# A one-layer attention and convolution trunk: the sums of a seven-product matrix form made earlier, a norm moved to other engines, and convolution taps ordered behind splits

## Chip, cores and metric

The kernel runs on one core of one Trainium2 chip. The metric is the device time of one execution in microseconds (us); three runs of the kernel before give a median of 1469.73.

## What is computed

One layer of a decoder on x of 1024 tokens x 1024 channels, in float32:

```python
h = rms_norm(x, attn_norm)
z = h @ w_in                                   # conv (512), q (768), six k/v parts (256 each), gates (36)
conv_out = conv_mixer(a_conv, ...)             # GLU, causal depthwise conv of width 31, LayerNorm, swish
kc, vc = compress(kc_r, ...), compress(vc_r, ...)
nsa_out = nsa_attention(q, kc, vc, ks, vs, kw, vw, gates)   # compressed, selected and window branches
x = x + concat([conv_out, nsa_out]) @ w_out
h = rms_norm(x, ffn_norm)
gate, up = split(h @ w_gate_up)                # 2 x 2816
x = x + (silu(gate) * up) @ w_down
return rms_norm(x, final_norm)
```

## The kernel before

**Products.** Every float32 product is made of three TensorE (PE) matmuls. Each operand is split into a high part, a cast by ScalarE (ACT), and a low part, the difference from it. `load_w` (L214) loads a weight tile, casts it (L225) and lets GpSimd (POOL) make the low part in four pieces of 128x256 (L229). `split` (L232) does the same for activations, with the subtraction on VectorE (DVE, L233). [...]

**Stages.** The 1024 tokens are worked in two halves of 512. First come the norm and the input projections of the first half: value projections, convolution input, compression of keys and values, queries. Two chains of side work run along there on DVE: the 31 convolution taps for each of two channel tiles (`conv_taps`, `cacc` at L601, fed by `taps_in`) and the splits and gates of the projections. Then attention runs, woven with fill work: the second half's projections, and the first half's output projection and feed-forward pairs. The feed-forward width of 2816 is 22 blocks of 128, worked as 11 pairs. A pair in the old form is `up_part` (four `gu` tiles of 24 matmuls, L1184, with `af` and `aw` made behind them at L1191 and L233) and `down_part` (eight `dn` tiles of 6 matmuls, L1203, each added to x by DVE at L1208).

**Around the change.** When attention is done, `second` makes the second half's output projection (`wo`, L1139, its weights loaded by `out_loads_k` at 256 KB each, ACT cast at L1065, POOL subtraction at L1068) and its feed-forward norm (`ffn_norm_in`: square on ACT, `rs` on DVE and POOL, the product x * rs * weight on DVE at L241, then PE transposes `tp` and their splits into `h`). It is woven with the first half's pairs. The first half's remaining pairs follow, and the second half's pair 0 in the old form. Its pairs 1 to 10 use a seven-product form (Winograd's variant of Strassen's): `wino_up` makes one block of gate and one of up from seven products of 256 tokens instead of eight (L1331, PSUM tiles `yy`, `zz`, `aa`). It needs four sums of quarters of h (`terms`, L1256 to L1263, each then split into `term`) and, for each block, four sums of weight quarters (`sum`, L1290), which `cut` splits into `w_s` (L1277; `w_g` is the split of the weight itself). `c` (L1346) is a sum of yy and a copy of zz; DVE must have made it before the next product goes on adding to yy. Between the products stand down matmuls of the pair before, six at a time.

The `terms` and the first `sum` tiles are written behind the last old-form pair of the first half; the scheduler places five of nine term operations ahead of it. Two buffers are used in turn, so that a sum waits for the split of the one before. Ahead of the first seven-product tile stand 36 down matmuls (`down_lead`, L1217: the first six of pair 0's eight tiles, interleaved).

**What sets the order.** PE's order in the seven-product form is written by hand. Elsewhere a list scheduler with its own time model places the instructions; `weave` mixes two generators by estimated durations, and `tc.issue_after` puts what follows behind a named instruction. On each engine the placed order is fixed, and an engine waits in it.

Of the kernel before, what the change touches and what calls it, by code (L numbers as in the profile page):

```python
# [19 lines left out]
P = 128  # L20
# [68 lines left out]
def tile_hymba(ctx: ExitStack, tc, x, attn_norm, w_in, conv_w, conv_b, conv_ln_g, conv_ln_b,  # L89
# [124 lines left out]
    def load_w(parts, a, b, eng=pool):  # L214
# [14 lines left out]
            eng.tensor_sub(lo[:, q], raw[:, q], hi[:, q].bitcast(F32))  # L229
        return (hi[:, :n].rearrange("p (k c) -> p k c", k=a), lo[:, :n].rearrange("p (k c) -> p k c", k=a))  # L230

    def split(hi, lo, src):  # L232
        return act.copy(hi, src), dve.tensor_sub(lo, src, hi.bitcast(F32))  # L233

    def norm_rows(dst, src, grow, p, tmp):
# [3 lines left out]
        dve.tensor_scalar(rs, ss, 1.0 / DM, EPS, op0=ALU.mult, op1=ALU.add)
        pool.tensor_tensor(rs, rs, mhalf, op=ALU.pow)  # L240
        dve.scalar_tensor_tensor(dst, src, rs, grow, op0=ALU.mult, op1=ALU.mult)  # L241
# [215 lines left out]
    def project_d(feed, dst, row, halves, scaled=False):  # L457
        wh, wl = feed.get()
        for hf in halves:
            o = acc_bank("zo")  # L460
            yield from gemm_t(o, wh, wl, hf)
            zh = p1.tile([P, 512], F32R, tag="zh", name="zh", bufs=2)
            zl = p1.tile([P, 512], F32R, tag="zl", name="zl", bufs=2)
            if scaled:
                sc = qsc[:, row // P:row // P + 1]
                act.mul(zh, o, sc)
                dve.scalar_tensor_tensor(zl, o, sc, zh.bitcast(F32), op0=ALU.mult, op1=ALU.subtract)
            else:
# [470 lines left out]

    def taps_in(n):  # L940
        taps = conv_taps(0)
        for _ in taps:
            yield n


# [111 lines left out]
            for kq in range(2) for ch in range(2) for c in range(2)]  # L1057

    def out_loads_k(p):
        def load(kt, ch):  # L1060
            raw = p.tile([P, 512], F32, tag="oraw", name="o_raw")
            hi = p.tile([P, 512], F32R, tag="ohi", name="o_hi", bufs=2)
            lo = p.tile([P, 512], F32R, tag="olo", name="o_lo", bufs=2)
            sp.dma_start(raw, w_out[0, kt * P:(kt + 1) * P, ch * 512:(ch + 1) * 512])
            act.copy(hi, raw)  # L1065
            for c in (0, 256):
                q = slice(c, c + 256)
                pool.tensor_sub(lo[:, q], raw[:, q], hi[:, q].bitcast(F32))  # L1068
            return hi, lo
        return [lambda kt=kq * 4 + k, ch=ch: load(kt, ch) for kq in range(2) for ch in range(2) for k in range(4)]  # L1070
# [83 lines left out]
    def ffn_norm_in(si, tag):  # L1154
        grow, xns = norm_space(acts[si])
        load_row(grow, ffn_norm[0])
        for t, x1 in enumerate(x1s[si]):
            xn = xns[t % 3]
            norm_rows(xn, x1, grow, pools[si], xn)
            yield 4.0  # L1160
            transpose_tile(xn, h2[si][0], h2[si][1], t * P, tag)
            yield 0.9

    banks, splits = [0], []
# [77 lines left out]
    def half(si, w, kh, th):  # L1242
        return h2[si][w][kh][:, :, th * 256:(th + 1) * 256]

    def wino_terms(si, p, tmp):
        def val(w, kh, th):
            return half(si, w, kh, th).bitcast(F32)
        x, y = (tmp[:, i, :].rearrange("p (k t) -> p k t", k=4) for i in range(2))

        def term(src):  # L1250
            h, l = [p.tile([P, 4, 256], F32R, tag="term", name="term", bufs=8) for _ in range(2)]
            split(h, l, src)
            return h, l

        def less(dst, src, kh, th):
            dve.tensor_sub(dst, src, val(0, kh, th))  # L1256
            dve.tensor_sub(dst, dst, val(1, kh, th))

        def from_(dst, kh, th, src):
            dve.tensor_sub(dst, val(0, kh, th), src)  # L1260
            dve.tensor_tensor(dst, dst, val(1, kh, th), op=ALU.add)

        dve.tensor_tensor(x, val(0, 0, 1), val(1, 0, 1), op=ALU.add)  # L1263
        less(y, x, 0, 0)
        t1 = term(y)
        from_(y, 1, 1, y)
        t2 = term(y)
        from_(x, 1, 1, x)
        t3 = term(x)
        from_(y, 1, 0, y)  # L1270
        t4 = term(y)
# [27 lines left out]
    def wino_load(f, p, q, raws=None, sums=None):  # L1299
        if raws is None:  # L1300
            raw = wp.tile([P, WCH], F32, tag="raw", name="g_raw", bufs=2)[:, :KT * P]
            raws = wino_raw(f, raw.rearrange("p (k c) -> p k c", k=KT),
                            (p, last["p"])[f % 2 == 0].tile([P, KT, P], F32, tag="uraw", name="u_raw"))
# [60 lines left out]
    def wino_ffn(fps, p, terms, ahead, down, behind):  # L1364
        loads = [lambda f=2 * fp + f2: wino_load(f, p, pd) for fp in fps for f2 in range(2)][1:]

        def down_load(f, own):
            if own:
                return load_w([(0, w_down[0, f * P:(f + 1) * P, :])], 1, DM, dve)
            raw = wp.tile([P, WCH], F32, tag="raw", name="d_raw", bufs=2)[:, :DM]  # L1370
            sp.dma_start(raw, w_down[0, f * P:(f + 1) * P, :])
            return [x.rearrange("p (o k) c -> p o (k c)", o=1)
                    for x in cut(p, raw.rearrange("p (k c) -> p k c", c=P), "g", 2)]
        for fp in fps:
            aws = new_aws((1,))
            wd = []
            for f2 in range(2):
                if loads:
                    with issue_after(behind):
                        ahead.append(loads.pop(0)())  # L1380
                    behind = []
                end = fp == fps[-1] and f2 == 1
                wd.append(down_load(2 * fp + f2, not end))
                wino_up(ahead.pop(0), terms, aws[1], f2, down, p, ALL, (6, 3, 3) if end else (6, 6, 6))
            run(down)
            down = down_part(wd, (1,), ALL, aws, fp == fps[-1])
        run(down)

# [45 lines left out]
    def fill_all():  # L1434
# [21 lines left out]
        for _ in range(NF // 2):  # L1456
            yield from ffn(feed, (0,), FT)

    def second(p):
        set_in(1, p)  # L1460
        set_norm(1, p)
        yield from out_proj_k(Feed(out_loads_k(p), 2), 1, ALL[:6])
        yield from ffn_norm_in(1, "t")

    BUFS = dict(k=1, v=1, q=2, pr=9, ph=3)
    def conv_rest():
# [4 lines left out]
    with ExitStack():  # L1471
# [15 lines left out]
    raws = wino_raw(2, base[:, :KT * P].rearrange("p (k c) -> p k c", k=KT),
                    last["p"].tile([P, KT, P], F32, tag="uraw", name="u_raw"))
    terms = wino_terms(1, last["p"], tmp)
    sums = list(wino_sums(*raws, pd))  # L1490
# [22 lines left out]
    p5_stack.close()
    pd_stack.close()
# [30 lines left out]
```

## Time and profile before

| what | us |
|---|---|
| three runs | 1472.3, 1466.56, 1469.73 (median 1469.73) |
| the profiled execution | 1464.45 |
| its span, first to last instruction | 1462.7 |
| PE busy in it | 1425.4 (97%) |
| DVE, ACT, POOL busy | 1029.5, 771.1, 698.5 |
| mean granted clock of PE | 0.994 |

The profiled execution is 5.28 us below the median of the runs, and 1.75 us of it lie outside the span. Rows of a timeline give start and duration in us, engine, line, operation and tiles; a bracket at the end gives the idle time before it and who ended it. A group's row gives a duration in ns. A mean over rows of a helper line such as L233 mixes many tiles.

### The profile page before, as it was taken

The numbers are of one execution on the slowest core, as the hardware profiler recorded it, in microseconds if no ns is written. First come the engines' busy times: TensorE is split into PE (matmuls) and PEld (weight loads), VectorE is DVE, ScalarE is ACT, GpSimd is POOL, SyncE is SP. The second block draws the span as 40 slices with busy tenths as digits, with TensorE's granted clock in tenths as the row PEclk, the third lists the DMA queues.
The fourth block names the chain that finished last, engine by engine and source line by source line (L and its number), as shares of the span: only waits on it lengthen the run. The fifth ranks groups of instructions, "written<-read, shape, count | busy, mean of one in ns | idle before, by whom it ended". The sixth has DMA issues, their size and how long they took to land.

```text
span 1462.7 us, 23496 instructions
## 1 busy us (share of the span) xinstructions
PE 1425.4 (97%) x7995; PEld 1231.0 (84%) x7995; DVE 1029.5 (70%) x2280; ACT 771.1 (53%) x1603; POOL 698.5 (48%) x977
## 2 busy tenths in 40 slices
PE   8999999999999999999999999999999999999997
PEld 7888888987778888888888888787887899999996
DVE  6893586779686768777587785412638988788884
ACT  6323566768675666766666664322425444444443
POOL 5677574767675546655665556645568000000001
PEclk9999999999999999999999999999999999999999
DMA  7236488567597244335335213734244423223311
GB/s 234 75 117 205 129 237 254 155 196 208 163 285 220 72 109 113 90 94 136 92 100 138 81 41 104 217 123 144 80 130 155 134 87 115 87 87 116 115 60 72
DMA packets 234246, 196.34 MB, mean 134 GB/s; under 512 B 14745, under 2 KB 204029, under 8 KB 234126
## 3 DMA queue, kind: packets, MB, share of 16 engines
q1 hardware_dynamic: 234126, 194.84, 45.1%
q8 instruction: 63, 1.03, 0.3%
q14 instruction: 57, 0.47, 0.1%
HBM read 161.04 MB, written 33.75 MB: 133 GB/s over the span
## 4 chain that ended last, share of the span: by engine, by line
PE 72%; DVE 9%; DMA 7%; POOL 6%; ACT 3%; issue 2%; SPq 1%; POOLq 0%; ACTq 0%; DVEq 0%
PE gu L1184 17%; PE dn L1203 14%; PE yy L1331 8%; PE pt L845 5%; PE zz L1331 4%; PE wo L1118 3%; POOL w_lo L229 3%; PE zo L145 3%; PE o L863 3%; PE s L818 3%; PE o L862 3%; DVE cacc L601 2%; PE vo L145 2%; DMA w_raw<-in_w_in_dram 2%; DMA o_raw<-in_w_out_dram 2%
## 5 line engine op out<-in xcount | busy, mean ns | idle before, releaser
L229 POOL TENSOR_TENSOR w_lo<-w_raw,w_hi 128x256 fp32r<-128x256 f32 (+1 forms) x508 | 411.9, 844 | 161.2 <-ACT w_hi L225 154.0
L1184 PE MATMUL gu<-h,w_hi 128*128 128x512 f32 x768 | 253.0, 398 | 0.6 <-DVE x L1208 0.6
L1203 PE MATMUL dn<-w_hi,aw 128*128 128x512 f32 x656 | 230.7, 397 | 1.6 <-DVE x L1208 1.2
L225 ACT CAST w_hi<-w_raw 128x1024 fp32r<-128x1024 f32 (+1 forms) x147 | 152.5, 1050 | 131.8 <-DMA w_raw<-in_w_in_dram 44.1
L839 POOL TENSOR_SCALAR pr<-pr,l,gates 128x640 f32<-128x640 f32 (+5 forms) x192 | 149.1, 791 | 119.2 <-DVE l L834 94.2
L233 DVE TENSOR_TENSOR pl<-pt,ph 128x384 fp32r<-128x384 f32 x264 | 140.3, 551 | 55.2 <-ACT ph L233 53.5
L829 ACT ACTIVATE pr<-pr,m 128x640 f32<-128x640 f32 (+5 forms) x192 | 141.4, 737 | 71.4 <-DVE m L826 69.6
L1184 PEld LDWEIGHTS gu<-h,w_hi 128*128 128x128 f32 x768 | 143.2, 188 | 29.5 <-DVE x L1208 1.0
L233 ACT CAST ph<-pt 128x384 fp32r<-128x384 f32 x264 | 118.6, 478 | 76.9 <-PE pt L845 60.4
L1413 POOL TENSOR_TENSOR rs<-rs,mhalf 128x1 f32<-128x1 f32 x4 | 2.6, 645 | 320.4 <-DVE rs L1412 320.2
L1184 PE MATMUL gu<-h,w_lo 128*128 128x512 f32 x384 | 152.3, 397 | 0.0
L1203 PEld LDWEIGHTS dn<-w_hi,aw 128*128 128x128 f32 x656 | 123.1, 188 | 27.5 <-DVE x L1208 2.1
L1208 DVE TENSOR_TENSOR x<-dn,x 128x512 f32<-128x512 f32 x168 | 113.4, 684 | 42.0 <-PE dn L1203 41.4
L845 PE MATMUL pt<-ident,pr 128*128 128x128 f32 x792 | 137.9, 274 | 2.3 <-DVE pl L233 1.2
L1203 PE MATMUL dn<-w_lo,aw 128*128 128x512 f32 x328 | 129.6, 395 | 0.0
L826 DVE CUSTOM_DVE_ANT_0 pr<-s,base 128x384 f32<-128x384 f32 (+3 forms) x192 | 101.2, 533 | 33.9 <-PE s L822 21.4
L845 PEld LDWEIGHTS pt<-ident,pr 128*128 128x128 f32 x792 | 102.2, 141 | 20.0 <-POOL pr L839 2.8
L145 PE MATMUL zo<-h,w_hi 128*128 128x512 f32 x320 | 106.0, 399 | 1.5 <-ACT w_hi L225 0.7
L1277 ACT CAST w_s<-sum 128x512 fp32r<-128x512 f32 x80 | 49.3, 621 | 108.3 <-PE yy L1331 90.5
L818 PE MATMUL s<-kt,q 128*128 128x384 f32 (+3 forms) x288 | 101.4, 354 | 3.6 <-DMA q<-q_d 1.6
L862 PE MATMUL o<-ph,vt 128*128 128x384 f32 x264 | 98.7, 374 | 2.3 <-ACT ph L233 1.9
L1331 PEld LDWEIGHTS yy<-term,w_s 128*128 128x128 f32 x720 | 93.8, 189 | 8.3 <-DVE c L1346 3.4
(275 smaller groups left out, 3156.9 us busy)
## 6 DMA issues: line engine op xcount, KB each, us to landing
w_raw<-in_w_gate_up_dram SPq DMA_DIRECT2D x48, 512.0 KB, 3.7
w_raw<-in_w_down_dram SPq DMA_DIRECT2D x43, 512.0 KB, 3.5
w_raw<-in_w_in_dram SPq DMA_DIRECT2D x40, 512.0 KB, 4.2
u_raw<-in_w_gate_up_dram SPq DMA_DIRECT2D x20, 512.0 KB, 4.9
g_raw<-in_w_gate_up_dram SPq DMA_DIRECT2D x19, 512.0 KB, 3.9
qc<-q_d SPq DMA_DIRECT2D x32, 192.0 KB, 3.9
pc_d<-pct SPq DMA_DIRECT2D x16, 384.0 KB, 3.7
pct<-pc_d SPq DMA_DIRECT2D x32, 192.0 KB, 2.7
```

Source lines behind the costliest of these rows:

```text
L145: lastpe[0] = pe.matmul(*args, **kw)
L225: act.copy(hi[:, :n], raw[:, :n])
L229: eng.tensor_sub(lo[:, q], raw[:, q], hi[:, q].bitcast(F32))
L233: return act.copy(hi, src), dve.tensor_sub(lo, src, hi.bitcast(F32))
L818: pe.matmul(sv, q2[0], kk_[:, 0, kk], start=True, stop=False)
L829: act.activation(pr[:, :n], pr[:, :n], AF.Exp, bias=m, scale=-1.0, accum_out=l3[:, r:r + 1])
L839: pool.tensor_scalar(x_, x_, l3[:, r2:r2 + 1], gates[:, i, c:c + 1], op0=ALU.mult, op1=ALU.mult)
L845: pe.transpose(pt[:, r * P:(r + 1) * P], prs[st][1 + r][:, kk * P:(kk + 1) * P], ident)
L862: pe.matmul(o[:, :384], v, ph, start=False, stop=False)
L1184: pe.matmul(o, w[:, k, :], h2[si][h][k // 4][:, k % 4, :], start=n == 0, stop=n == 3 * KT - 1)
L1203: pe.matmul(o, aws[si][:, a, k, t * P:(t + 1) * P], b[:, 0, ch * 512:(ch + 1) * 512], start=n == 0, stop=n == 5)
L1331: pe.matmul(o, w[:, k, :], h[:, k, :], start=fresh and n == 0, stop=n == 11, skip_group_check=not fresh)
```

## The change

It has five parts.

1. **Sums early.** `wino_terms` no longer splits: it makes four separate sums, in tiles of the second half's `act` space. It is called with the first weight sums from a new function `ahead_of_form`, ahead of the first half's last pair. The splits (`wino_split`) stay where they were.
2. **Second norm.** For the second half, DVE's one product of x, rs and the weight is replaced by an ACT multiplication by rs and a POOL multiplication by the weight row, both 128x1024. The row is loaded at the start of `second`, into a tile of its own.
3. **Output weights** are loaded in pairs of k tiles (512 KB), in turn into the `uraw` buffer and `base`.
4. **Taps.** Each step of the first half's taps is ordered behind the latest low part of a split, or the latest `zl` of a projection.
5. **Start of the form.** `down_lead` isn't used: the down matmuls of pair 0 follow the first products six at a time. The down weights of pair 1 are loaded when those are through, and fewer loads stand ahead.

The diff, cut:

```diff
+    lastlo = [None]
+
     def split(hi, lo, src):
-        return act.copy(hi, src), dve.tensor_sub(lo, src, hi.bitcast(F32))
+        pair = act.copy(hi, src), dve.tensor_sub(lo, src, hi.bitcast(F32))
+        lastlo[0] = pair[1]
+        return pair
...
-        dve.scalar_tensor_tensor(dst, src, rs, grow, op0=ALU.mult, op1=ALU.mult)
+        if aside:
+            act.mul(dst, src, rs)
+            pool.tensor_mul(dst, dst, grow)
+        else:
+            dve.scalar_tensor_tensor(dst, src, rs, grow, op0=ALU.mult, op1=ALU.mult)
...
         taps = conv_taps(0)
-        for _ in taps:
+        while True:
+            with tc.issue_after(lastlo[0].ins):
+                if next(taps, None) is None:
+                    return
             yield n
...
         def load(kt, ch):
-            raw = p.tile([P, 512], F32, tag="oraw", name="o_raw")
+            if kt % 2 == 0:
+                if kt % 4 == 0:
+                    pair = p.tile([P, 2, 512], F32, tag="uraw", name="o_raw")
+                else:
+                    pair = base[:, :DM].rearrange("p (k c) -> p k c", k=2)
+                sp.dma_start(pair, w_out[0, kt * P:(kt + 2) * P, ch * 512:(ch + 1) * 512]
+                             .rearrange("(k p) c -> p k c", p=P))
+                pairs.append(pair)
+            raw = pairs[-1][:, kt % 2, :]
...
-            sp.dma_start(raw, w_out[0, kt * P:(kt + 1) * P, ch * 512:(ch + 1) * 512])
...
-        x, y = (tmp[:, i, :].rearrange("p (k t) -> p k t", k=4) for i in range(2))
+        t3, t1, t2, t4 = [tmp[:, i, :].rearrange("p (k t) -> p k t", k=4) for tmp in tmps for i in range(2)]
...
+        dve.tensor_tensor(t3, val(0, 0, 1), val(1, 0, 1), op=ALU.add)
+        less(t1, t3, 0, 0)
+        from_(t2, 1, 1, t1)
+        from_(t3, 1, 1, t3)
+        from_(t4, 1, 0, t2)
+        return t1, t2, t3, t4
...
-                if loads:
+                if loads and len(ahead) < 2:
...
-                wd.append(down_load(2 * fp + f2, not end))
+                if fp != fps[0]:
+                    wd.append(down_load(2 * fp + f2, not end))
...
             run(down)
+            if fp == fps[0]:
+                ahead.append(loads.pop(0)())
+                wd = [down_load(2 * fp + f2, True) for f2 in range(2)]
...
+    def ahead_of_form():
+        assert not out_left
+        early["raws"] = wino_raw(2, base[:, :KT * P].rearrange("p (k c) -> p k c", k=KT),
+                                 pd.tile([P, KT, P], F32, tag="uraw", name="u_raw"))
+        early["terms"] = wino_terms(1, [acts[1].tile([P, 2, DM], F32, tag="act", name="terms", bufs=2)
+                                        for _ in range(2)])
+        with issue_after(normed):
+            early["sums"] = list(wino_sums(*early["raws"], pd))
...
+        grow = py.tile([P, 2, 542], F32, tag="y", name="grow").rearrange("p a b -> p (a b)")[:, :DM]
+        load_row(grow, ffn_norm[0])
...
-    with issue_after([gone] + splits):
-        ahead = [wino_load(2, p4, pd, raws, sums)]
+    behind = [gone] + splits
+
+    with issue_after([gone]):
+        ahead = [wino_load(2, p4, pd, early["raws"], early["sums"])]
...
-        down = down_lead(wd, 1, aws)
-        some(down, 36)
-        wino_ffn(range(1, NF // 2), p4, terms, ahead, down, [gone] + splits)
+        down = down_part(wd, (1,), ALL, aws)
+        wino_ffn(range(1, NF // 2), p4, terms, ahead, down, behind)
```

**DVE behind the second norm.** The place is the end of the second half's transposes, beside the first half's pair 9 (L1191 `af` and `aw` of its two blocks; `h_11222` to `h_11225` are the second half's normed rows, high and low). Before:

```order
L233 TENSOR_TENSOR aw<-af,aw 128x512
L233 TENSOR_TENSOR h_11224<-tp,h_11222 128x4x128
L233 TENSOR_TENSOR h_11225<-tp,h_11223 128x4x128
L1263 TENSOR_TENSOR terms<-h_11222,h_11224 128x1024
L1256 TENSOR_TENSOR terms<-terms,h_11222 128x1024
L1257 TENSOR_TENSOR terms<-terms,h_11224 128x1024
L1260 TENSOR_TENSOR terms<-h_11223,terms 128x1024
L1261 TENSOR_TENSOR terms<-terms,h_11225 128x1024
L1191 TENSOR_TENSOR af<-gu,af 128x512
L233 TENSOR_TENSOR aw<-af,aw 128x512
L1208 TENSOR_TENSOR x_5749<-dn,x_5749 128x512 x4
L1208 TENSOR_TENSOR x_5750<-dn,x_5750 128x512 x4
```

After (L235 is the split, L1275 to L1282 are the terms, L1313 the weight sums):

```order
L235 TENSOR_TENSOR aw<-af,aw 128x512
L1282 TENSOR_TENSOR terms<-h_11222,h_11224 128x1024
L235 TENSOR_TENSOR h_11225<-tp,h_11223 128x4x128
L1313 TENSOR_TENSOR sum<-u_raw 128x512
L1313 TENSOR_TENSOR sum<-base,u_raw 128x512
L1275 TENSOR_TENSOR terms<-terms,h_11222 128x1024
L1313 TENSOR_TENSOR sum<-sum,base 128x512
L1276 TENSOR_TENSOR terms<-terms,h_11224 128x1024
L1279 TENSOR_TENSOR terms<-h_11223,terms 128x1024
L1313 TENSOR_TENSOR sum<-base,sum 128x512
L1279 TENSOR_TENSOR terms<-h_11223,terms 128x1024
L1280 TENSOR_TENSOR terms<-terms,h_11225 128x1024
```

Five of nine term sums stood here; now all nine do, and the four weight sums. Behind these rows come `af`, one more term sum, the second `aw` of the pair, two more, and then the eight additions x<-dn. In PE's order 47 gu matmuls stand between the last transposes and the first dn of pair 9 (before, 31), and 33 dn matmuls between the last wo and the first transpose (before, 13 dn and 21 gu).

**DVE in the first half's compression.** `af` and `al` are the activated hidden rows of compressed keys and the low parts of their split, which the product kc needs; `xl` are low parts of the input, `zl` those of projections. Before:

```order
L601 SCALAR_TENSOR_TENSOR cacc<-y,cols,cacc 128x512 x3
L467 SCALAR_TENSOR_TENSOR zl<-zo,qsc,zh 128x512 x2
L520 TENSOR_SCALAR bc<-h_975 128x1
L520 TENSOR_SCALAR bc<-h_976 128x1
L522 TENSOR_SCALAR af<-h_975,bc 128x256
L498 SCALAR_TENSOR_TENSOR af<-af 128x256
L522 TENSOR_SCALAR af<-h_976,bc 128x256
L233 TENSOR_TENSOR al<-af,ah 128x256
L233 TENSOR_TENSOR xl<-cols,xh 128x8 x2
L498 SCALAR_TENSOR_TENSOR af<-af 128x256
L233 TENSOR_TENSOR al<-af,ah 128x256
L467 SCALAR_TENSOR_TENSOR zl<-zo,qsc,zh 128x512 x2
```

After (L609 are the taps):

```order
L506 SCALAR_TENSOR_TENSOR af<-af 128x256
L235 TENSOR_TENSOR xl<-cols,xh 128x8
L609 SCALAR_TENSOR_TENSOR cacc<-y,cols,cacc 128x512
L235 TENSOR_TENSOR xl<-cols,xh 128x8
L530 TENSOR_SCALAR af<-h_976,bc 128x256
L235 TENSOR_TENSOR al<-af,ah 128x256
L609 SCALAR_TENSOR_TENSOR cacc<-y,cols,cacc 128x512
L506 SCALAR_TENSOR_TENSOR af<-af 128x256
L609 SCALAR_TENSOR_TENSOR cacc<-y,cols,cacc 128x512
L235 TENSOR_TENSOR al<-af,ah 128x256
L609 SCALAR_TENSOR_TENSOR cacc<-y,cols,cacc 128x512
L475 SCALAR_TENSOR_TENSOR zl<-zo,qsc,zh 128x512 x2
```

Before, no tap stood between the first activation of `af` (L498) and the last `al`; now three do. The first xl of the stage, which stood behind 12 of the first channel tile's taps, has none ahead.

**POOL in the second norm.** `rs` is the norm's power, `rows` the normed row, `w_lo` the pieces of weights. Before:

```order
L1068 TENSOR_TENSOR o_lo<-o_raw,o_hi 128x256 x4
L229 TENSOR_TENSOR w_lo<-w_raw,w_hi 128x256 x4
L1068 TENSOR_TENSOR o_lo<-o_raw,o_hi 128x256 x6
L240 TENSOR_TENSOR rs<-rs,mhalf 128x1 x3
L229 TENSOR_TENSOR w_lo<-w_raw,w_hi 128x256 x8
L240 TENSOR_TENSOR rs<-rs,mhalf 128x1
L229 TENSOR_TENSOR w_lo<-w_raw,w_hi 128x256 x51
L240 TENSOR_TENSOR rs<-rs,mhalf 128x1 x2
```

After (L247 is the multiplication by the weight row):

```order
L1088 TENSOR_TENSOR o_lo<-base,o_hi 128x256 x4
L229 TENSOR_TENSOR w_lo<-w_raw,w_hi 128x256 x4
L244 TENSOR_TENSOR rs<-rs,mhalf 128x1 x3
L247 TENSOR_TENSOR rows<-rows,grow 128x1024 x3
L244 TENSOR_TENSOR rs<-rs,mhalf 128x1
L229 TENSOR_TENSOR w_lo<-w_raw,w_hi 128x256 x8
L247 TENSOR_TENSOR rows<-rows,grow 128x1024
L229 TENSOR_TENSOR w_lo<-w_raw,w_hi 128x256 x48
```

Three products of 128x1024 stand in one piece behind the last output weights, and the fourth behind eight pieces of w_lo.

More of the change, by code (lines that the diff above doesn't have):

```diff
@@ L230, in load_w, with norm_rows @@
         return (hi[:, :n].rearrange("p (k c) -> p k c", k=a), lo[:, :n].rearrange("p (k c) -> p k c", k=a))
+    lastlo = [None]
     def split(hi, lo, src):
[L233 to L235 removed]
+        pair = act.copy(hi, src), dve.tensor_sub(lo, src, hi.bitcast(F32))
+        lastlo[0] = pair[1]
+        return pair
+    def norm_rows(dst, src, grow, p, tmp, aside=False):
         ss = p.tile([P, 1], F32, tag="ss", name="ss", bufs=4)
@@ L466, in project_d @@
                 act.mul(zh, o, sc)
-                dve.scalar_tensor_tensor(zl, o, sc, zh.bitcast(F32), op0=ALU.mult, op1=ALU.subtract)
+                lastlo[0] = dve.scalar_tensor_tensor(zl, o, sc, zh.bitcast(F32), op0=ALU.mult, op1=ALU.subtract)
             else:
@@ L1059, in out_loads_k @@
     def out_loads_k(p):
+        pairs = []
         def load(kt, ch):
-            raw = p.tile([P, 512], F32, tag="oraw", name="o_raw")
+            if kt % 2 == 0:
[7 more added lines that the diff above has]
+            raw = pairs[-1][:, kt % 2, :]
             hi = p.tile([P, 512], F32R, tag="ohi", name="o_hi", bufs=2)
             lo = p.tile([P, 512], F32R, tag="olo", name="o_lo", bufs=2)
-            sp.dma_start(raw, w_out[0, kt * P:(kt + 1) * P, ch * 512:(ch + 1) * 512])
             act.copy(hi, raw)
@@ L1152, in norm_space, with ffn_norm_in @@
         return a[:, 0, :], (a[:, 1, :], b[:, 0, :], b[:, 1, :])
-    def ffn_norm_in(si, tag):
-        grow, xns = norm_space(acts[si])
-        load_row(grow, ffn_norm[0])
+    normed = []
+    def ffn_norm_in(si, tag, grow=None):
+        row, xns = norm_space(acts[si])
+        if grow is None:
+            grow = row
+            load_row(grow, ffn_norm[0])
         for t, x1 in enumerate(x1s[si]):
             xn = xns[t % 3]
-            norm_rows(xn, x1, grow, pools[si], xn)
+            norm_rows(xn, x1, grow, pools[si], xn, si == 1)
             yield 4.0
-            transpose_tile(xn, h2[si][0], h2[si][1], t * P, tag)
+            normed[:] = transpose_tile(xn, h2[si][0], h2[si][1], t * P, tag)
             yield 0.9
@@ L1243, in half, with wino_terms @@
         return h2[si][w][kh][:, :, th * 256:(th + 1) * 256]
-    def wino_terms(si, p, tmp):
+    def wino_terms(si, tmps):
         def val(w, kh, th):
             return half(si, w, kh, th).bitcast(F32)
-        x, y = (tmp[:, i, :].rearrange("p (k t) -> p k t", k=4) for i in range(2))
[L1250 to L1253, printed above, removed]
+        t3, t1, t2, t4 = [tmp[:, i, :].rearrange("p (k t) -> p k t", k=4) for tmp in tmps for i in range(2)]
         def less(dst, src, kh, th):
@@ L1261, in from_, with wino_split, term @@
             dve.tensor_tensor(dst, dst, val(1, kh, th), op=ALU.add)
[L1263 to L1271, printed above, removed]
+        dve.tensor_tensor(t3, val(0, 0, 1), val(1, 0, 1), op=ALU.add)
[4 more added lines that the diff above has]
+        return t1, t2, t3, t4
+    def wino_split(si, p, sums):
+        def term(src):
+            h, l = [p.tile([P, 4, 256], F32R, tag="term", name="term", bufs=8) for _ in range(2)]
+            split(h, l, src)
+            return h, l
+        t1, t2, t3, t4 = [term(src) for src in sums]
         b11, b21, b22 = [tuple(half(si, w, kh, th) for w in range(2)) for kh, th in ((0, 0), (1, 0), (1, 1))]
@@ L1302, in wino_load @@
             raws = wino_raw(f, raw.rearrange("p (k c) -> p k c", k=KT),
-                            (p, last["p"])[f % 2 == 0].tile([P, KT, P], F32, tag="uraw", name="u_raw"))
+                            (p, pd)[f % 2 == 0].tile([P, KT, P], F32, tag="uraw", name="u_raw"))
         raw, uraw = raws
@@ L1455, in fill_all @@
         yield from ffn_norm_in(0, "z")
-        for _ in range(NF // 2):
+        for n in range(NF // 2):
+            if n == NF // 2 - 1:
+                ahead_of_form()
             yield from ffn(feed, (0,), FT)
+    def ahead_of_form():
[6 more added lines that the diff above has]
+            early["sums"] = list(wino_sums(*early["raws"], pd))
+    early, out_left = {}, [1]
     def second(p):
@@ L1461, in second @@
         set_norm(1, p)
+        grow = py.tile([P, 2, 542], F32, tag="y", name="grow").rearrange("p a b -> p (a b)")[:, :DM]
+        load_row(grow, ffn_norm[0])
         yield from out_proj_k(Feed(out_loads_k(p), 2), 1, ALL[:6])
-        yield from ffn_norm_in(1, "t")
+        yield from ffn_norm_in(1, "t", grow)
+        out_left.clear()
     BUFS = dict(k=1, v=1, q=2, pr=9, ph=3)
@@ L1481, in tile_hymba @@
         run(fill)
-    tmp = acts[1].tile([P, 2, DM], F32, tag="act", name="terms", bufs=2)
     last["p3"].close()
     p5_stack, last["p"] = open_pool("p5", "right")
[L1487 to L1490, printed above, removed]
+    terms = wino_split(1, last["p"], early["terms"])
     two = acts[0].tile([P, 2, DM], F32, tag="act", name="rows", bufs=2)
```

## The prediction

> **What bounds the kernel now.** I read the page's first part, then PE's waits, then the windows of the places that the change touches, then their timelines and the groups by tile.
>
> ```profile
> span 1462.7 us, 23496 instructions
> ...
> PE 1425.4 (97%) x7995; PEld 1231.0 (84%) x7995; DVE 1029.5 (70%) x2280; ACT 771.1 (53%) x1603; POOL 698.5 (48%) x977
> ```
>
> TensorE (PE) sets the time. The change alters none of its products, so it can act only on the 1462.7 − 1425.4 = 37.3 us in which PE is idle, and on stretches of lowered clock. PE's waits (us in total, times, longest) say which idle time lies at the places changed; the wait for mix is there for comparison.
>
> ```profile
> PE yy L1331 <- DVE c L1346: 3.0, 2, 1.9
> PE wo L1118 <- DMA mix<-mix_d: 2.3, 1, 2.3
> ...
> PE h L145 <- ACT xh L233: 1.8, 1, 1.8
> ...
> PE vo L145 <- DVE gates L301: 0.8, 1, 0.8
> ...
> PE gu L1184 <- DVE x L1208: 0.6, 1, 0.6
> ...
> PE wo L1139 <- ACT o_hi L1065: 0.2, 1, 0.2
> ...
> PE dn L1203 <- DVE rs L239: 0.2, 1, 0.2
> ```
>
> In the windows, the busy times stand in the order PE, PEld, DVE, ACT, POOL; the number behind them is PE's granted clock.
>
> ```profile
> 80.00:100.00 20.00, 17.46 (x116) 15.96 (x116) 19.58 (x34) 5.17 (x11) 11.61 (x11) 1.00 0.38 126
> 460.00:480.00 20.00, 17.68 (x93) 15.13 (x92) 12.31 (x38) 9.61 (x22) 5.82 (x8) 0.91 0.66 193
> 1060.00:1080.00 20.00, 20.00 (x88) 16.19 (x87) 8.74 (x12) 5.32 (x6) 13.37 (x17) 1.00 0.34 105
> 1100.00:1120.00 20.00, 19.45 (x84) 15.46 (x83) 18.15 (x23) 11.26 (x16) 16.92 (x16) 1.00 0.26 79
> 1120.00:1140.00 20.00, 20.00 (x99) 16.74 (x98) 18.05 (x22) 9.66 (x15) 10.11 (x10) 1.00 0.70 237
> 1140.00:1160.00 20.00, 17.73 (x140) 17.01 (x138) 19.28 (x32) 10.78 (x18) 0.00 (x0) 1.00 0.42 132
> 1160.00:1180.00 20.00, 19.31 (x127) 18.28 (x128) 17.36 (x31) 8.85 (x16) 0.00 (x0) 0.91 0.39 115
> ```
>
> From 1100 to 1160 VectorE (DVE) is busy 18 to 19 us in each 20: it is the engine that PE waits for where the seven-product form begins. At 1060 to 1080 it has 11 us free. The change moves work from the one place to the other.
>
> **Part 1: the start of the seven-product form (gain).** PE's timeline has the waits, and its pitch: the 31 products from 1052.80 to 1060.07 take 7.27 / 31 = 0.234 us each.
>
> ```profile
> 1052.80 0.71 PE L1184 MATMUL gu<-h,w_hi 128*128 128x512 f32 x2
> ...
> 1060.07 0.40 PE L1203 MATMUL dn<-w_hi,aw 128*128 128x512 f32 x1
> ...
> 1105.29 0.50 PE L1184 MATMUL gu<-h,w_hi 128*128 128x512 f32 x1 [0.55 <-DVE x L1208]
> ...
> 1148.53 1.69 PE L1331 MATMUL yy<-term,w_s 128*128 128x256 f32 x12 [1.05 <-DVE c L1346]
> ...
> 1160.69 1.73 PE L1331 MATMUL yy<-term,w_s 128*128 128x256 f32 x9 [1.91 <-DVE c L1346]
> ```
>
> Idle are 0.55 + 1.05 + 1.91 = 3.5 us. The clock of 0.91 in the window behind the last adds (1 − 0.91) × 20 = 1.8. Behind the 2.3 us wait for mix the window shows 0.91 too; with the 1.8 at 80 to 100 it shows 1.00. [...]
>
> What goes from DVE here are four weight sums and four of the term sums. The tile views give them (ns: least, median, most), and DVE's timeline the end of the stretch:
>
> ```profile
> L1260 DVE TENSOR_TENSOR terms<-h,terms x3: 1632/1649/1766, 1058.6 to 1112.4; 128x1024 f32<-128x1024 f32 x3
> ...
> L1263 DVE TENSOR_TENSOR terms<-h,h x1: 1215/1215/1215, 1054.5 to 1054.5; 128x1024 f32<-128x1024 f32 x1
> ```
> ```profile
> L1290 DVE TENSOR_TENSOR sum<-base,u_raw x1: 1226/1226/1226, 1100.6 to 1100.6; 128x512 f32<-128x512 f32 x1
> ...
> L1290 DVE TENSOR_TENSOR sum<-base,sum x1: 674/674/674, 1107.6 to 1107.6; 128x512 f32<-128x512 f32 x1
> ```
> ```profile
> 1109.89 1.27 DVE L1208 TENSOR_TENSOR x<-dn,x 128x512 f32<-128x512 f32 x2
> ...
> 1122.18 3.35 DVE L241 SCALAR_TENSOR_TENSOR x<-x,rs,rows 128x1024 f32<-128x1024 f32 x2
> ...
> 1127.95 0.69 DVE L1191 TENSOR_TENSOR af<-gu,af 128x512 f32<-128x512 f32 x1 [1.26 <-PE gu L1184]
> ...
> 1130.58 1.21 DVE L1277 TENSOR_TENSOR w_g<-base,w_g 128x1024 fp32r<-128x1024 f32 x1
> ```
>
> That is about 4 × 1.23 + 4 × 1.65 = 11.5 us out of a stretch where DVE is full, so c comes in time. In exchange the 36 leading down products (36 × 0.234 = 8.4 us of PE) no longer stand ahead of the first yy, which is now due at the end of gu, near 1127.9. Its w_g was ready at 1130.58 + 1.21 = 1131.8, which is 6.3 behind the last norm operation (1122.18 + 3.35). The norm can now begin right behind the last eviction (1111.2) rather than behind sums and splits, some 6 us sooner, so w_g is ready near 1126: an estimate, with 2 us to spare. Taken: **−5.3**; at worst c or w_s comes late once and a wait of 1.9 with its 1.8 stays: −1.6.
>
> **Part 2: the second half's projection and norm.** PE waited 0.2 for o_hi and 0.2 for rs. w_out now comes in pairs, half as many DMAs on SP's queue. Taken: **−0.4** (0 to −0.6). The norm's multiplications change engine; their cover is PE's work up to the transposes.
>
> ```profile
> 1034.31 0.39 PE L1184 MATMUL gu<-h,w_hi 128*128 128x512 f32 x1
> ...
> 1034.82 1.28 DVE L241 SCALAR_TENSOR_TENSOR rows<-x,rs,rows 128x1024 f32<-128x1024 f32 x1 [1.33 <-DMA rows<-in_ffn_norm_dram]
> ...
> L233 ACT CAST term<-terms x4: 1039/1046/1051, 1095.2 to 1115.7; 128x1024 fp32r<-128x1024 f32 x4
> ...
> L1068 POOL TENSOR_TENSOR o_lo<-o_raw,o_hi x32: 722/740/752, 919.8 to 1027.0; 128x256 fp32r<-128x256 f32 x32
> ```
>
> The last wo ended 13 products ahead of 1034.31, near 1031.3. Without the DMA wait of 1.33 (the weight row is loaded early now) the first row was ready at 1034.8, 3.5 behind it. Its 1.28 is replaced by ScalarE's 1.05 and by GpSimd's (POOL's) 4 × 0.74 = 2.96, estimated from the quarter-size pieces: 6.2. In the new order the first transpose stands 33 products behind the last wo, 7.7 us: 1.5 to spare, and by the same count 2.1, 3.5 and 2.7 for the other tiles. So it is hidden, at nothing; without that cover see the first rival.
>
> **Part 3: the sums made early (loss).** Between the first half of the last split of h and the second aw of pair 9, DVE now also does seven term sums and four weight sums.
>
> ```profile
> 1053.27 1.29 DVE L233 TENSOR_TENSOR h<-tp,h 128x512 fp32r<-128x512 f32 x2 [1.76 <-ACT h L233]
> ...
> 1063.31 1.28 DVE L233 TENSOR_TENSOR aw<-af,aw 128x512 fp32r<-128x512 f32 x1 [0.69 <-ACT aw L233]
> ```
>
> In the new order 47 products stand between the last transposes and dn: 11.0 us. The first h of the last tile ends 1053.27 + 0.65 − 1052.80 = 1.1 behind their start, so dn starts 9.9 behind that h, and the products that need the second aw come 24 later, at 15.5. DVE's chain in that time: one h (0.65), one af (0.68), two aw (0.8 each), seven terms, four sums. With 1.22 and 0.68 it is 2.9 + 8.5 + 2.7 = 14.1: no wait. With 1.66 and 1.23 it is 2.9 + 11.6 + 4.9 = 19.4: PE waits 3.9. In before, terms in this place took both, so I take means of the rows' ends, 1.50 (nearer the slow ones, since POOL is 13 of 20 us busy at 1060) and 0.95: 2.9 + 10.5 + 3.8 = 17.2. Taken: **+1.7** (0 to 3.9, and 1.8 more if the clock falls).
>
> **Part 4: the first half's taps.** They now follow the latest split, so what PE waits for comes first: the 1.8 for xh and the 0.8 for gates go, −2.6. In return three taps stand in the chain ahead of the last al, which kc needs.
>
> ```profile
> L601 DVE SCALAR_TENSOR_TENSOR cacc<-y,cols,cacc x62: 710/752/1277, 42.2 to 896.6; 128x512 f32<-128x512 f32 x62
> ...
> 131.69 0.42 DVE L233 TENSOR_TENSOR al<-af,ah 128x256 fp32r<-128x256 f32 x1 [0.47 <-ACT ah L233]
> ...
> 131.74 0.28 PE L539 MATMUL kc<-ah,w2h 128*128 128x256 f32 x1
> ```
>
> kc began 0.05 behind the start of al, so there is no slack: three taps cost 3 × 0.75 = 2.3 to 3 × 1.28 = 3.8, or nothing if af comes as much sooner. Half the gain is taken: **−1.3** (−2.6 to +1.2).
>
> **Sum.** −5.3 − 0.4 + 1.7 − 1.3 = −5.3. The profiled execution took 1464.45 (span 1462.7), 5.3 below the median of the runs, 1469.73. It becomes 1459.15, and as a median **1464.4**. About 0.5%, 7.3 us, is what a measurement of this kernel can tell from no change: faster is below 1462.4, slower above 1477.1.
>
> **Rivals.** *Slower: GpSimd's norm products are stretched.* If DVE's work beside them makes each longer by e, PE, whose transposes stand in its fixed order, waits 4e − 2.7 in all. Pieces of w_lo beside the taps show what e could be:
>
> ```profile
> L229 POOL TENSOR_TENSOR w_lo<-w_raw,w_hi x45: 731/1182/1982, 35.7 to 111.9; 128x256 fp32r<-128x256 f32 x37, 128x274 fp32r<-128x274 f32 x8
> ```
>
> At the median a product takes 4 × 1.18 = 4.7: e = 1.8, a wait of 4.5, time 1468.9. At the most it takes 7.9: e = 5.0, a wait of 17.3 and two lowered clocks, 3.6, which make 15.6 of loss: 1485. It turns slower than before at 4e − 2.7 = 5.3, a product of 5.0 us, and by over 0.5% at 6.8. Against it: DVE's work there mostly reads PSUM (x<-dn, h<-tp), and o_lo beside such work stayed at 0.74. Chance 0.08.
>
> *Gain eaten: DVE and GpSimd exclude each other wholly.* Each sum of part 3 waits for a whole w_lo piece: 2.9 + 7 × (1.22 + 0.74) + 4 × (0.68 + 0.74) = 22.3, a wait of 6.8 with a lowered clock, 8.6 in place of 1.7: 1471.3, and 1472.6 with nothing from part 4. [...] The terms' 1.65 is 0.43 over 1.22, some 0.6 of a piece, so the trace bears it out only in part. Chance 0.15.
>
> *More gain: both unknown costs vanish.* The chain of part 3 only has to shrink from 17.2 to 15.5, and part 4 to keep its 2.6: −8.3, time 1461.4. Chance 0.31, with what lies beyond.
>
> *The change doesn't do what it says:* the waits at yy stay, because c is late by its own chain on PE and ScalarE; part 1 gives 0.55, time 1469.2. Chance 0.06.
>
> **How the numbers follow.** The forecast, 1462.4 to 1468.5, has 0.40. The range goes down 3 us past the case of more gain, 1458.5, and up to the eaten gain, 1472.5; outside are most of the stretched norm and the ends of the two cases, 0.2. Faster is the case of more gain, 0.31; slower most of the first rival and a little of the second, 0.07; the rest is 0.62.
>
> **What would show it.** Right: no wait for c at the first yy products, and a clock of 1.00 behind them; none for xh near 85; a wait of 1 to 4 us at dn for aw some 15 us behind the last h; transposes without a wait for rows. Wrong: POOL products over 5.0 us, a wait at yy for w_g or w_s, a wait at kc over 2.6.

## The result, and the profile after

The changed kernel took 1459.38 us against 1467.85 of the kernel before (medians of 6 runs each), a ratio of 0.9943 with a 95% interval from 0.9923 to 0.9964: 8.5 us less. Measured again in the study, 1458.57 against 1467.68, 0.9940 (0.9924 to 0.9956), 9.1 us less. The forecast was 5.3 less, "same" by the bound of 0.5%; both measurements lie just beyond that bound, with intervals that reach across it, and inside the range, in the case called more gain.

The two profiled executions are only 4.0 us apart (1464.45 and 1460.47), so their difference has to be read by stages. These are PE's waits in the kernel after, in the same view as before:

```profile
PE pt L853 <- DVE pl L235: 3.3, 2, 2.5
PE wo L1138 <- DMA mix<-mix_d: 3.0, 1, 3.0
...
PE dn L1227 <- DVE x L1232: 1.3, 2, 0.8
...
PE kc L547 <- ACT ah L235: 1.1, 1, 1.1
...
PE kc L547 <- DVE al L235: 0.7, 1, 0.7
...
PE dn L1227 <- DVE af L1215: 0.5, 2, 0.3
...
PE dn L1227 <- DVE aw L235: 0.2, 1, 0.2
```

The waits of yy for c (3.0), gu for x (0.6), h for xh (1.8) and vo for gates (0.8) are gone, and so are those for o_hi and rs. New are two waits at kc, 1.8 in all. The wait of pt for pl, in the attention, is 2.1 longer than before (3.3 for 1.2), but it swings from 0.7 to 5.1 in the traces of this study, with the old parts and with the new, so I don't lay it to the change. The waits of dn for aw (0.2) and of dn for x lie elsewhere than at pair 9. The windows after, and ahead of them the one at 120 of the kernel before:

```profile
120.00:140.00 20.00, 19.70 (x87) 15.57 (x87) 7.08 (x14) 7.98 (x14) 13.44 (x21) 1.00 0.75 205
```
```profile
80.00:100.00 20.00, 20.00 (x135) 18.70 (x135) 17.33 (x26) 5.90 (x9) 12.01 (x13) 1.00 0.46 148
...
120.00:140.00 20.00, 17.95 (x78) 13.89 (x77) 14.63 (x21) 8.90 (x15) 14.87 (x21) 1.00 0.62 182
...
1060.00:1080.00 20.00, 19.80 (x86) 15.64 (x86) 16.31 (x17) 5.32 (x6) 17.06 (x15) 1.00 0.35 105
...
1120.00:1140.00 20.00, 20.00 (x123) 17.79 (x123) 17.55 (x23) 10.09 (x18) 7.62 (x7) 1.00 0.59 172
1140.00:1160.00 20.00, 20.00 (x139) 18.55 (x138) 18.30 (x33) 10.21 (x18) 0.00 (x0) 1.00 0.40 125
1160.00:1180.00 20.00, 20.00 (x143) 18.72 (x142) 16.19 (x27) 8.18 (x15) 0.00 (x0) 1.00 0.40 113
```

PE is full from 1120 to 1180, at a clock of 1.00. DVE gave 16.3 us of 20 at 1060 to 1080 (8.7 before) and PE lost 0.2 there. The window at 120 holds the price of the taps: PE has 17.95 us of 20 there, 19.70 before.

Two starts of PE products cut the time in three: the first gu of the feed-forward part, and the first aa of the sixth seven-product block, when the form runs steadily. Before, then after:

```profile
519.73 0.39 PE L1184 MATMUL gu<-h,w_hi 128*128 128x512 f32 x1
...
1216.08 1.12 PE L1331 MATMUL aa<-h,w_g 128*128 128x256 f32 x8
```
```profile
521.08 0.39 PE L1208 MATMUL gu<-h,w_hi 128*128 128x512 f32 x1
...
1211.40 0.88 PE L1354 MATMUL aa<-h,w_g 128*128 128x256 f32 x6
```

The middle takes 1216.08 − 519.73 = 696.35 before and 690.32 after, 6.0 less; from there to the start of the last product it is 238.59 in both. From that start to the end of the span it is 8.06 before and 8.78 after. The front (start to gu) came out 1.35 longer. It is the part that varies: q, mix, the values and the weights come by DMA there, and its length in the traces of this study runs from 517 to 526. These two lengths in every kernel:

| kernel | front | middle |
|---|---|---|
| before | 519.73 | 696.35 |
| changed; again | 521.08; 517.81 | 690.32; 690.15 |
| taps_only | 521.89 | 695.95 |
| form_only | 523.96 | 693.85 |
| form_and_outputs | 522.98 | 692.38 |
| all_but_taps | 523.29 | 690.48 |
| norm_only | 522.85 | 700.49 |
| all_but_outputs | 517.07 | 693.44 |
| old_start | 520.54 | 693.94 |
| old_sums | 523.84 | 694.51 |
| taps_held; taps_faster | 526.27; 526.22 | 690.06; 690.03 |
| one_sum_twice | 518.66 | 696.11 |

The middle of norm_only is longer for reasons of that one execution, which took 3.5 more than the median of its runs: `wo` waited 2.3 for mix there (0.4 in before), and the clock was lowered once behind that, to half.

The end goes with one part alone, the paired output weights. Without them, in five traces, it takes 8.06 or 8.07 from the start of the last product; with them, in nine, 8.62 to 8.85: the last transfers of the output are issued some 0.3 later and land 0.6 to 0.8 later. Why isn't shown.

### The profile page after: what moved, and what is told of

Read it like the earlier page. It is cut to its first block, busy times and chain, and to the rows that moved or that the text cites. A ratio compares the mean times of both kernels' runs of the same rounds, so it can differ in the third digit from the quotient of the medians.

```text
span 1458.8 us, 23485 instructions
## 1 busy us (share of the span) xinstructions
PE 1422.4 (98%) x7995; PEld 1229.6 (84%) x7995; DVE 1029.5 (71%) x2276; ACT 776.4 (53%) x1607; POOL 702.8 (48%) x981
## 4 chain that ended last, share of the span: by engine, by line
PE 79%; DMA 6%; DVE 6%; POOL 4%; ACT 2%; issue 2%; SPq 1%; ACTq 0%; POOLq 0%; DVEq 0%
PE gu L1208 17%; PE dn L1227 16%; PE yy L1354 8%; PE pt L853 5%; PE zz L1354 4%; PE zc L145 3%; PE wo L1159 3%; PE wo L1138 3%; DMA w_raw<-in_w_in_dram 3%; PE o L870 3%; PE o L871 3%; PE s L826 3%; POOL w_lo L229 2%; PE vo L145 2%; PE zo L145 2%; PE aa L1354 2%
## 5 line engine op out<-in xcount | busy, mean ns | idle before, releaser
L1227 PE MATMUL dn<-w_hi,aw 128*128 128x512 f32 x688 | 242.1, 397 | 2.1 <-DVE x L1232 1.3
L235 DVE TENSOR_TENSOR pl<-pt,ph 128x384 fp32r<-128x384 f32 x264 | 140.4, 551 | 56.7 <-ACT ph L235 54.8
L235 ACT CAST ph<-pt 128x384 fp32r<-128x384 f32 x264 | 118.8, 478 | 80.9 <-PE pt L853 61.8
L1227 PEld LDWEIGHTS dn<-w_hi,aw 128*128 128x128 f32 x688 | 129.1, 188 | 29.6 <-DVE x L1232 2.2
L1232 DVE TENSOR_TENSOR x<-dn,x 128x512 f32<-128x512 f32 x176 | 119.2, 686 | 28.9 <-PE dn L1227 28.1
L1227 PE MATMUL dn<-w_lo,aw 128*128 128x512 f32 x344 | 136.0, 395 | 0.0
```

Source lines behind the costliest of these rows:

```text
L235: pair = act.copy(hi, src), dve.tensor_sub(lo, src, hi.bitcast(F32))
L1227: pe.matmul(o, aws[si][:, a, k, t * P:(t + 1) * P], b[:, 0, ch * 512:(ch + 1) * 512], start=n == 0, stop=n == 5)
```

## The experiments

The theory was that the gain is made at the start of the seven-product form and the taps give back most of what they win. The rivals: the gain beyond the forecast is the taps'; the early sums cost what was forecast; the norm was a cost of its own.

**The parts alone.** Each kernel is before with some parts, or after without some: the hunks of the diff above are taken or left. Each is scheduled anew, so that it differs from its neighbours in PE's order too: between the last wo and the first transpose PE has 13 dn and 21 gu in before, 33 dn in the changed kernel, 21 dn in form_and_outputs and 43 gu in form_only and all_but_outputs. The worth of a part is what the scheduler made of it as well. The us behind a ratio are worked out from the ratio; by the medians they differ by up to 0.8. taps_only takes `lastlo` and `taps_in`:

> The kernel before with part 4 alone (taps ordered behind the latest split). Theory (the gain is made at the start of the seven-product form; the taps give back most of what they win): the waits for xh (1.76) and gates (0.79) near 85 us go, waits at kc of about 1.8 us appear near 128, sum -0.7 us; the waits at yy of 3.0 us and the lowered clock behind them stay. Rival A (the measured gain beyond the forecast, some 3 us, is the taps' doing, in the attention part): -4 us or more, and less PE idle time between 230 and 480 us than before.

1464.77 us, 0.9986 (0.9973 to 0.9998), 2.1 less. The waits at kc came (1.0 and 0.8), those for xh and gates went. The middle is as before. The gain lies between the two numbers, and its interval (−4.0 to −0.3) holds 0.7 and ends at 4. Rival A's other sign didn't come: PE was idle for 13.0 us between 230 and 480, 10.8 in before.

> The kernel before with parts 1 and 5 alone (sums early, new start of the form). Theory: -5.1 us: no wait at yy (3.0), none at gu for x (0.55), clock 1.00 from 1100 to 1180 (1.7), and 0.2 lost at dn in pair 9. Rival A: the same places in the trace, but the time falls by less than 3 us because the rest of the gain is the taps'. Rival B (the early sums cost what the forecast said): a wait of 1.5 to 3.9 us at dn for the second aw, time -3 to -1.

1464.49 us, 0.9979 (0.9966 to 0.9992), 3.1 less, not 5.1. No wait for c, and neither dn nor gu waits for the early sums; but the projection of the second half now waits for its weights:

```profile
PE wo L1139 <- ACT o_hi L1065: 1.9, 3, 1.1
```

That is 2 of the 5 us, which no theory had said. (By the medians the whole gain is 2.3.)

> The kernel before with part 2 alone (second norm's products on ScalarE and GpSimd, its weight row loaded early). Theory: -0.2 us, no more than noise; GpSimd's products of 128x1024 take 2.4 us, PE's transposes wait for no row; the waits for o_hi and o_lo stay. Rival C (the norm on DVE was a cost of its own in the kernel before, since DVE is late at the start of the form): -2 us or more, with smaller waits at yy.

1468.21 us, 1.0006 (0.9992 to 1.002): nothing, as the theory said. The waits for c are still there (3.8).

> The changed kernel with the taps ordered as before. Theory: -5.6 us against the kernel before (form 5.1, norm and output weights 0.5), the waits for xh and gates near 85 us are back (2.5), no wait at kc. Rival A: -4 us or less, since the taps' 4 us are missing.

1460.48 us, 0.9961 (0.9945 to 0.9976), 5.7 less (−8.1 to −3.5): the theory's number, though the interval just holds rival A's 4 too. The waits for xh (1.8) and gates (0.8) are back, and kc waits 0.4. The middle is that of the changed kernel, so its 6 us aren't the taps'. What is left for the taps is the 2.7 to 3.1 us between this kernel and the changed one, from two series of runs: too rough to decide between 0.7 and 4.

**What norm and output weights are for.** form_and_outputs is form_only with w_out in pairs, all_but_outputs the changed kernel with w_out singly.

```diff
-            raw = pairs[-1][:, kt % 2, :]
+            raw = p.tile([P, 512], F32, tag="oraw", name="o_raw")
+            sp.dma_start(raw, w_out[0, kt * P:(kt + 1) * P, ch * 512:(ch + 1) * 512])
```

> The kernel before with parts 1, 3 and 5 (early sums, new start, output weights in pairs), norm and taps as before. Theory (the early sums alone made the second half's projection wait for o_hi, 1.9 us, because its weights came singly, and part 3 is there to take that away): the o_hi waits are below 0.5 us in all, and the time is 5 to 6 us below the kernel before, like that of the kernel with all but the taps. Rival (it was the norm that repaired it): o_hi waits of 1.5 us or more stay, time -3 to -4 us.

1463.59 us, 0.9968 (0.9954 to 0.9981), 4.7 less, between the two numbers. No wait for o_hi is left, but the norm on DVE is now late: the last wo starts 503.4 behind the first gu of the feed-forward part, 510.9 in before, and 21 products cover the norm where 34 did:

```profile
PE tp L248 <- DVE rows L241: 1.5, 1, 1.5
```

> The changed kernel with its output weights loaded singly, as before. Theory (early sums with single loads make the projection wait for o_hi): o_hi waits of 1.5 to 2.5 us at 1010 to 1030 us, time 1.5 to 2.5 us above the changed kernel. Rival (the norm moved off VectorE removes them too): o_hi waits under 0.5 us, time as the changed kernel.

1460.59 us, 2.0 above the changed kernel run beside it; 0.9958 (0.9943 to 0.9974) against before. Theory: the waits are back,

```profile
PE wo L1150 <- ACT o_hi L1076: 1.9, 2, 1.2
```

and a wait of 0.7 for c with them. So the norm (part 2 of the change), nothing by itself, is worth 1.9 us in the middle (692.38 to 690.48) once the form's parts and the paired weights are there. The paired weights (part 3) are worth 3.3 in the middle (693.44 to 690.15) and cost 0.6 at the end (8.06 to 8.63); by the runs they are worth 2.0, little beside a spread of some 6 us in each.

**Sums or start.** old_start is the changed kernel with the leading down products and the order of loads of before, and with the form's first weight splits ordered behind the last aw, as they were (`splits` holds that aw):

```diff
-    with issue_after([gone]):
+    with issue_after([gone] + splits):
...
+        down = down_lead(wd, 1, aws)
+        some(down, 36)
```

> The changed kernel with the start of the form as before (36 leading down products, loads as before), sums early. Theory A (the sums on VectorE were the cause): VectorE has 11 us less to do there, so the waits for c shrink from 3.0 us to under 1 and no lowered clock follows; time within 2 us of the changed kernel. Theory B (the lead used up the down products that should cover c): waits for c of 2 us or more stay, with a clock of 0.91 behind them; 3 to 5 us slower than the changed kernel.

1464.92 us, 0.9977 (0.9962 to 0.9992), and the waits for c are 3.2: theory A has fallen. The lowered clock that theory B had behind them didn't come: the clock was 1.00 from 1140 to 1180. DVE, rid of the sums, did not use the time. Its timeline in old_start, then in the changed kernel:

```profile
1127.58 0.69 DVE L1215 TENSOR_TENSOR af<-gu,af 128x512 f32<-128x512 f32 x1 [8.75 <-PE gu L1208]
1128.96 0.69 DVE L235 TENSOR_TENSOR aw<-af,aw 128x512 fp32r<-128x512 f32 x1 [0.69 <-ACT aw L235]
...
1129.91 1.22 DVE L1300 TENSOR_TENSOR w_g<-base,w_g 128x1024 fp32r<-128x1024 f32 x1 [0.26 <-ACT w_g L1300]
```
```profile
1119.62 1.54 DVE L1300 TENSOR_TENSOR w_g<-base,w_g 128x1024 fp32r<-128x1024 f32 x1
...
1128.23 0.69 DVE L1215 TENSOR_TENSOR af<-gu,af 128x512 f32<-128x512 f32 x1 [0.38 <-PE gu L1208]
1129.61 0.69 DVE L235 TENSOR_TENSOR aw<-af,aw 128x512 fp32r<-128x512 f32 x1 [0.69 <-ACT aw L235]
```

In old_start DVE is idle for 8.75 us and only then starts the weight splits, which stand behind the last aw, and c comes late. In the changed kernel the same w_g stands ahead of that aw, ten us sooner. Theory B had the place right (the start). Whether its reason (down products used up too soon) is the one isn't shown: old_start changes the lead, the order of the loads and the place of the weight splits together, and they were not tried apart.

> The changed kernel with the term sums made as before, in two buffers with the splits between them (weight sums where the scheduler puts them), and the new start. Theory A (the sums were the cause): the first yy is due 8.4 us earlier while VectorE still makes the last terms, so PE waits 2 to 6 us at the first yy or zz products and at gu for x, time 3 to 6 us above the changed kernel. Theory B (the lead was the cause): waits below 1 us, time within 2 us of the changed kernel.

It has the old `wino_terms` and the new start. 1464.89 us, 0.9977 (0.9962 to 0.9993), and the middle 4.2 longer than in the changed kernel. PE's new waits:

```profile
PE dn L1227 <- DVE rs L243: 1.5, 1, 1.5
...
PE dn L1227 <- ACT aw L235: 1.1, 1, 1.1
PE yy L1355 <- DVE w_g L1301: 1.1, 1, 1.1
```

The last two are at the form (1133 and 1138), 2.2 us of the 2 to 6 that theory A had. The first is at 1030.75, in the second norm, ahead of any sum; why it came isn't shown. So each half of the change at the form does less without the other.

**How near the early sums are to costing.** one_sum_twice makes one sum's two operations twice:

```diff
         less(t1, t3, 0, 0)
+        less(t1, t3, 0, 0)
```

> The changed kernel with two of the nine term operations done twice (3.3 us more of VectorE's time ahead of the additions x<-dn of pair 9; the sums come out the same). Theory (the early sums fit with next to nothing to spare: the first addition ended 0.14 us ahead of the gu product that needs its bank): PE waits about 3.1 us for x at the gu products behind pair 9, 3 us slower than the changed kernel, 1.7 more if the clock falls. Rival (the scheduler's cover there is wide): a wait of under 1 us.

1462.07 us, 3.5 above the changed kernel beside it; 0.9962 (0.9947 to 0.9976) against before. PE's wait is the 3.1 that was expected, and the window of this kernel shows the clock at 0.83 behind it:

```profile
PE gu L1208 <- DVE x L1232: 3.1, 1, 3.1
```
```profile
1060.00:1080.00 20.00, 16.68 (x60) 12.73 (x59) 16.90 (x17) 2.72 (x3) 15.54 (x12) 0.83 0.35 105
```

(1 − 0.83) × 20 = 3.4 more: 6 us in this trace for 3.3 us of work on an engine that is idle elsewhere. The sums fit, with nothing to spare.

**The taps.** taps_held keeps taps out of the last quarter of the compression, until its low parts are made:

```diff
         while True:
+            if hold[0]:
+                yield n
+                continue
```

> The changed kernel, with the taps held back from the last quarter of the keys' compression until its low parts are made. Theory (the three taps ahead of al cost what PE waits at kc): the waits at kc fall from 1.8 us to below 0.6, the stage up to kc is 1 to 1.7 us shorter than in the changed kernel; over the whole time the same or 1 to 2 us faster, which the spread of the attention part may hide. Rival (kc waits for ScalarE, which stands behind the weights' DMA): waits at kc of 1.2 us or more stay.

1464.49 us, 0.9973 (0.9961 to 0.9985): slower than the changed kernel. The waits at kc are gone in full, as the theory said, and another took their place:

```profile
PE sc L668 <- DMA qc<-q_d: 3.6, 1, 3.6
```

taps_faster has `taps_in(2.0)` in place of 2.7:

> The changed kernel with the taps emitted every 2.0 us of the planned time and not every 2.7, so that two taps stand ahead of the last al and fewer behind it. Theory: the wait at kc falls from 1.8 us to about 1, no wait for xh comes back near 85, and the part from kc to the attention is 1 us shorter since fewer taps stand beside it; 1 to 2 us faster than the changed kernel. Rival: VectorE, 17 of 20 us busy at 80 to 100 already, is late for xh or gates there; 1 us or more slower.

1460.75 us, 2.2 above the changed kernel beside it (0.9951, 0.9936 to 0.9965, against before). The waits at kc stayed (1.1 and 0.7), those for xh did not come back, and zo waited 2.0 for w_hi. Neither is better than what the change has.

**The changed kernel again,** for its interval (given at the top):

> The changed kernel again, to narrow its interval and to stand on one chip with the three beside it. From the traces (6.0 us less between the first feed-forward product and the end, 0.8 less ahead of it, as means over kernels with and without the ordered taps): -6 to -7.5 us against the kernel before. If the first measurement of -8.4 was right in full: -8 or more.

No version in the study beats it.

## Why the prediction was right or wrong

The parts here are numbered as in the prediction: 1 the start of the form, 2 the projection and the norm, 3 the early sums, 4 the taps.

**Part 1, −5.3:** right in size. In the two profiles 0.55 + 1.05 + 1.91 of waiting are gone, and the lowered clock. Its 1.8 for the clock was of that one execution: of the four traces with the old start, before (a wait of 1.9, a clock of 0.91 over 1160 to 1180) and norm_only (2.8) have the lowered clock behind the second wait, taps_only (2.4) and old_start (2.4, a clock of 1.00) do not. The reason was in part wrong. I put the gain down to the 11.5 us taken from DVE; old_start takes them too and keeps the waits. What the trace shows instead is that the weight splits no longer stand behind the last aw; how much of the gain is theirs isn't shown (see old_start). My estimate had w_g ready near 1126; it was 1121.2 (1119.62 + 1.54), with that order.

**Part 2, −0.4:** right for the sum (no wait for o_hi, rs or rows), with the wrong picture behind it. These parts are no small gain of their own; they take away two waits, 1.9 for o_hi and 1.5 for rows, that other parts bring (form_only, form_and_outputs). What the paired weights add at the end of the kernel, 0.6, has no term in the forecast. GpSimd's product took less than 4 × 0.74:

```profile
1028.85 7.12 POOL L247 TENSOR_TENSOR rows<-rows,grow 128x1024 f32<-128x1024 f32 x3 [0.30 <-ACT rows L246]
...
1042.04 2.40 POOL L247 TENSOR_TENSOR rows<-rows,grow 128x1024 f32<-128x1024 f32 x1
```

2.4 us each, half of the 5.0 from which the first rival decides; that rival is out.

**Part 3, +1.7: the step that failed.** DVE's chain came as worked out, the time at which PE needs its end did not. DVE's timeline in the changed kernel, then PE's:

```profile
1050.64 0.69 DVE L235 TENSOR_TENSOR h<-tp,h 128x512 fp32r<-128x512 f32 x1 [0.95 <-ACT h L235]
...
1066.97 1.23 DVE L235 TENSOR_TENSOR aw<-af,aw 128x512 fp32r<-128x512 f32 x1
1068.12 1.76 DVE L1279 TENSOR_TENSOR terms<-h,terms 128x1024 f32<-128x1024 f32 x1
1069.92 1.64 DVE L1280 TENSOR_TENSOR terms<-terms,h 128x1024 f32<-128x1024 f32 x1
1071.49 4.86 DVE L1232 TENSOR_TENSOR x<-dn,x 128x512 f32<-128x512 f32 x8
```
```profile
1060.74 0.40 PE L1227 MATMUL dn<-w_hi,aw 128*128 128x512 f32 x1
...
1065.96 0.50 PE L1227 MATMUL dn<-w_hi,aw 128*128 128x512 f32 x1 [0.20 <-DVE af L1215]
...
1072.31 0.41 PE L1208 MATMUL gu<-h,w_hi 128*128 128x512 f32 x1
```

From the first h (1051.3) to the end of aw (1068.2) are 16.9 us, 17.2 forecast; dn starts 9.4 behind h, 9.9 forecast. But the products at 24 behind dn's start need only the high part of aw, which ScalarE casts from af; the scheduler put the low part's products 13 later, 3.0 us, so PE needed the end of the chain at 18.5 and not at 15.5. PE waited 0.2 there, at the first product of the eighth dn tile: by the view for af itself, not for aw. What was next was the addition x<-dn, done at about 1072.17 for a gu at 1072.31. I had it as no bound; with 3.3 us more of terms it became one, in one_sum_twice.

**The rival of whole exclusion:** the terms took 1.21 to 1.77 beside GpSimd's pieces, at most 0.56 over, never a whole piece of 0.74, and the wait of 6.8 did not come. GpSimd's pieces were stretched as well, to some 1.72 beside a slow term. A slow term and a piece together took 1.69, from one term's start to the next, where 1.21 and 0.74 one after the other make 1.95 and side by side 1.21. So the trace of after shows such an exclusion only in part, as that of before did.

**Part 4, −1.3:** right as far as PE's idle time goes. The waits for xh and gates went, and the price came, at 1.8 (1.3 in the second trace) where the three taps were put at 2.3 to 3.8. Over this stage PE was busy for, before and after:

```profile
60.00:200.00 140.00, 134.39 (x734) 115.12 (x734) 91.68 (x184) 58.71 (x149) 90.98 (x118) 1.00 0.51 153
```
```profile
60.00:200.00 140.00, 135.28 (x735) 115.94 (x734) 105.91 (x198) 58.26 (x148) 91.55 (x119) 0.99 0.53 155
```

It is 133.9 to 134.7 in the five traces with the old taps and 135.2 to 136.2 in seven with the new ones (without taps_held and taps_faster): 1.3 more in the mean, in groups that don't overlap. The runs have more, but can't tell it from that: taps_only gives −2.1 (−4.0 to −0.3). So have the fronts: means of 522.6 and 520.1, −2.4, in groups that spread by 4 and 7 us. The clock could be a part of it: behind the xh wait it is lowered, to half, near 87 us in three of the five old ones (form_only, norm_only, form_and_outputs), not in before, from whose 1.00 I worked; of the seven new ones two have it, behind the wait at kc (taps_only, old_sums). But over the whole front the lowered clock costs both groups the same, 6.5 and 6.3 us in the mean. The rest isn't settled.

**The sum:** the middle has −6.0 where the forecast has −5.3 − 0.4 + 1.7 = −4.0, and 1.5 of these 2.0 are the cost of the early sums that didn't come. The front has −2.4 where it has −1.3, and the end +0.6 where it has nothing. Together they make −7.8; the runs have −8.5 and −9.1, with intervals that hold it. That the rival of more gain, 1461.4, came nearest is in part luck. It asked for the two costs to vanish: that of the early sums did, though the chain didn't shrink to 15.5, but the wait at kc came.

## What to carry to other kernels

When work is moved to a place where an engine is idle, count what waits for it there product by product: high and low parts of one operand can be due several us apart (3.0 here), and the next thing in that engine's queue (here the additions x<-dn, with 0.14 us) may have less room than the work itself. A wait that is taken away brings the next one forward: the sums, the projection's loads and the norm paid in full only together (3.1, 4.7 and 5.7 us as they were added), so parts of such a change should not be judged alone. And an idle engine beside a late operation (8.75 us here) can point to the order, not to load.

## What the runs showed of the hardware

**The lowered clock has a raster.** In each of the 14 traces every stretch of half clock (0.50), up to the final norm, starts on a grid of 3.413 us that is fixed in that trace and lasts one or two steps of it. I counted PE's idle time in each step of that grid, from the first record of the clock (14.5 us in before) on. Of 30 steps with 1.9 us or more all were followed by a half-clock step, of 51 with 1.2 to 1.9 us 23, and of 125 with 0.7 to 1.2 us 2. In before the step from 1157.98 to 1161.39 has PE busy for 1.50 us, and the clock behind it is 0.50 until 1164.81. The waits of 2.4 us in taps_only and old_start lie across a grid line and left the clock alone, while the one of 1.9 in before lies within a step and lowered it.

**One product of 128x1024 on GpSimd took 2.40 us** in the changed kernel, less than four pieces of 128x256 at 0.74 (2.96).
